# A seven-product MLP in fp32 on one core: the seventh product in split parts, a base block copied by GpSimd, the weights' sums held behind the tokens' square sums

## The chip, the cores and the metric

One core of a Trainium2 chip. The metric is device time in microseconds of one execution of the whole program (lower is better). Five engines run their own queues of instructions in order and wait for one another by semaphores: TensorE (PE), VectorE (DVE), ScalarE (ACT), GpSimd (POOL) and SyncE (SP), which here only issues transfers.

## The reference

A two-layer encoder trunk on 256 tokens of width 1024: layer 0 mixes tokens by neighbourhood and latent attention, layer 1 by dilated windows, and each is followed by an MLP with squared ReLU. All in float32.

```python
def sq_relu_mlp(xn, w1, w2):
    return jnp.square(jax.nn.relu(xn @ w1)) @ w2      # w1: 1024 x 4096, w2: 4096 x 1024

def reference(x, ...):
    for layer in range(2):
        xn = rms_norm(x, norm_mix[layer])
        x = x + (even_mixer if layer % 2 == 0 else odd_mixer)(xn, ...)
        x = x + sq_relu_mlp(rms_norm(x, norm_mlp[layer]), mlp_w1[layer], mlp_w2[layer])
    return rms_norm(x, norm_final)
```

## The kernel before

The tokens stay in SBUF, features on partitions (`x`, 8 blocks of 128 features by 256 tokens). The weights are streamed from HBM in chunks of up to 128 x 2048, in the order of one list (`specs`). The program has four phases in time: the even mixer, the first MLP, the odd mixer, the second MLP.

*Split products.* A float32 product is made of three passes in the format fp32r: each operand is split into a rounded part `hi` (a cast on ACT, L197) and the rest `lo` (a subtraction on DVE, L198), and `mm3` (L201 to L203) adds up hi x hi, hi x lo and lo x hi in PSUM. `split` does the one, `load_weight` and `split_piece` bring each chunk of weights: loads go up to four chunks ahead, splits up to two (`weight`). Three buffers hold split weights, four hold raw ones.

*The MLP* runs over 16 hidden chunks of 256. `up(j)` multiplies chunk j (48 matmuls of 128x256, weights stationary), then ReLU (L365) and square (L367). `down(j)` multiplies the hidden chunk by its second weights into eight PSUM banks of 128 tokens x 512 outputs. The order is up 0, 1, 2, down 0, up 3, down 1, and so on; a period is one up and one down. `beside` slips four transposes into some downs of the second MLP (L482).

*Seven products.* For the first 14 chunks the 2 x 2 x 2 block product (token halves x hidden halves x output halves) is done with seven products (`SEVEN`) instead of eight, after Strassen and Winograd. They need sums of hidden blocks (L373 to L375) and sums of blocks of weights. A weight chunk holds blocks 0, 1 and 2 as loaded; block 3 is the base of the sums:

- `sums` (two blocks): SP loads the base block into both (L139, 512 KB), then GpSimd issues a DMA that adds blocks 0 and 2 to them in memory (L140).
- `more_sums`: DVE adds block 0 to the second of the sums (L172, written over `raw`'s free fourth block) and block 1 to that (L173, the tile `every`).
- `split_sums` splits the two `sums` into `sumh` and `suml`, as one more step of `split_piece`.

Six products are three passes each. The seventh, Q4, is a single float32 matmul of `whole` (the unsplit square of one hidden block, L372) with the unsplit `every` (L389); the profile shows it as two matmuls. The last two chunks use plain products (`EIGHT`).

*The start of an MLP* is `hand_over`: for each quarter of the features, once its projection is done, DVE adds it to `x` (L300), ACT and DVE make `xh` and `xl` of the normed tokens (`prepare`, L237 and L238), and at the end `add_squares` forms the sums of squares of the tokens (L243 to L247). Their inverse root is applied after the down products, so TensorE can begin `up(0)` with the first quarters.

*Order.* Within these phases a scheduler sets each engine's order by the program's order, priorities and its own estimate of when inputs are ready; it can put an instruction ahead of earlier ones. `tc.high_priority` raises a block's instructions; `tc.issue_after(ins)` keeps a block's instructions on `ins`'s engine behind `ins`. On the engine itself the order is then fixed.

*Buffers that the change touches.* Tiles of tag `quarter` (four, shared with the mixers) hold the split hidden chunks `hh`; `hl` has three buffers of six blocks; `xt` (tokens first, 2 x 1024 columns) belongs to the last MLP.

Of the kernel before, what the change touches and what calls it, by code (L numbers as in the profile page):

```python
# [19 lines left out]
F32 = mybir.dt.float32  # L20
F32R = mybir.dt.float32r
AF = mybir.ActivationFunctionType
ALU = mybir.AluOpType
# [3 lines left out]
P = 128  # L27
D = 1024
KT = D // P
T = 256  # L30
NT = T // P
# [10 lines left out]
BLK = 512  # L42
# [7 lines left out]
def trunk(ctx, tc, a, out):  # L50
# [76 lines left out]
    plan_mlp(1)  # L127

    parts = {}
    state = {"loaded": 0, "split": (0, 0), "used": 0, "pool": None}  # L130

    def load_weight(pieces=1, before=lambda i: None):
        j = state["loaded"]
        src, n, _, seven = specs[j]
        if seven:

            blocks = src.rearrange("p (b n) -> p b n", n=BLK)
            sums = state["pool"].tile([P, 2, BLK], F32, tag="sum", name="sum", bufs=3)
            nc.sync.dma_start(sums, blocks[:, 3:4, :].broadcast_to([P, 2, BLK]))  # L139
            nc.gpsimd.dma_start(sums, blocks[:, 0:3:2, :], accum_op=ALU.add)  # L140
            n = 3 * BLK
        raw = wraw.tile([P, WCH], F32, tag="raw", name="raw")
# [11 lines left out]
    def split_piece(eng=None):  # L154
        j, i = state["split"]
        _, _, n, seven = specs[j]
        state["split"] = (j, i + 1) if i < n - (not seven) else (j + 1, 0)
        if i == 0:
            parts[j][1:3] = (wsp.tile([P, WCH], F32R, tag=v, name=v) for v in ("whi", "wlo"))
            if seven:  # L160
                more_sums(parts[j])
        if i == n:
            parts[j][1:3], (raw, hi, lo) = split_sums(parts[j])
            return split(hi, lo, raw)
        raw, hi, lo = (z[:, cut(j, i, n)] for z in parts[j][:3])
        return split(hi, lo, raw, eng)

    def more_sums(part):

        raw, sums = part[0].rearrange("p (b n) -> p b n", n=BLK), part[3]  # L170
        every = state["pool"].tile([P, BLK], F32, tag="every", name="every", bufs=2)
        nc.vector.tensor_tensor(raw[:, 3, :], sums[:, 1, :], raw[:, 0, :], op=ALU.add)  # L172
        nc.vector.tensor_tensor(every, raw[:, 3, :], raw[:, 1, :], op=ALU.add)  # L173
        part.append(every)

    def split_sums(part):
        _, hi, lo, sums, every = part
        more = [state["pool"].tile([P, 2, BLK], F32R, tag=v, name=v, bufs=2) for v in ("sumh", "suml")]
        blocks = lambda z, t: [z[:, b * BLK:(b + 1) * BLK] for b in range(4)] + [t[:, b, :] for b in range(2)]
        return [blocks(hi, more[0]) + [every], blocks(lo, more[1])], (sums, *more)  # L180

    def prefetch(loads, splits):
        while state["loaded"] < min(loads, len(specs)):
# [56 lines left out]
    def add_squares(b, s):  # L240

        q = scratch([2, T], "q") if b else two(s)
        nc.scalar.activation(q, x[:, 2 * b:2 * b + 2, :], AF.Square)  # L243
        if b:
            nc.vector.tensor_tensor(two(s), two(s), q, op=ALU.add)
        if b == 3:
            nc.vector.tensor_tensor(s[:, 0:T], s[:, 0:T], s[:, T:2 * T], op=ALU.add)  # L247

    def columns(s):

# [41 lines left out]
    def hand_over(accs, last, n):  # L292

        xT = half_tile(act, "xh", 2), half_tile(act, "xl", 2)
        s = sum_tile()
        for b in range(4):
            last[b]()
            v, acc = x[:, 2 * b:2 * b + 2, :], two(accs[b])
            with tc.high_priority(NORM_PRIO):
                nc.vector.tensor_tensor(v, acc, v, op=ALU.add)  # L300
                for f in zip(*(prepare(k, n, xT) for k in (2 * b, 2 * b + 1))):
                    done = [step() for step in f]

        with tc.issue_after(done[0]), tc.issue_after(done[1]):
            for b in range(4):
                add_squares(b, s)
        return xT, s

    def open_accs():
# [31 lines left out]

    SEVEN = (("P1", 5, 0), ("P2", 4, 1), ("Q3", 0, 2), ("Q6", 1, 3), ("Q5", 3, 4), ("Q7", 2, 5), ("Q4", None, 6))

    EIGHT = {"P2": ((1, 0), (0, 1)), "Q3": ((1, 3), (0, 2)), "C22": ((3, 3), (2, 2)), "Q4": ((3, 0), (2, 1))}

    def mlp(mp, xT, s, apart=(), beside=lambda j, p: None):

        hs = {}

        def up(j, pu):
            w = weight()

            ranges = [range(4), range(4, 6), range(6, 8)] if j == 0 else [range(8)]
            for ks in ranges:
# [6 lines left out]
            nc.scalar.activation(r, pu, AF.Relu)  # L365
            h = mp.tile([P, 8, P], F32, tag="h", name="h", bufs=1)
            nc.scalar.activation(h[:, 4:8, :].rearrange("p (t f) n -> p f t n", f=2), r.rearrange("p (f t n) -> p f t n", f=2, t=2), AF.Square)  # L367
            hh = act.tile([P, KT // 2, T], F32R, tag="quarter", name="hh", bufs=4).rearrange("p a (b n) -> p (a b) n", n=P)
            hl = mp.tile([P, 6, P], F32R, tag="hl", name="hl", bufs=3)
            if j < 14:  # L370
                whole = mp.tile([P, P], F32, tag="whole", name="whole", bufs=3)
                nc.scalar.activation(whole, r[:, P:2 * P], AF.Square)  # L372
                nc.vector.tensor_tensor(h[:, 2:4, :], h[:, 7:8, :].broadcast_to([P, 2, P]), h[:, 5:7, :], op=ALU.subtract)  # L373
                nc.vector.tensor_tensor(h[:, 1, :], h[:, 5, :], h[:, 3, :], op=ALU.subtract)
                nc.vector.tensor_tensor(h[:, 0, :], h[:, 4, :], h[:, 1, :], op=ALU.subtract)  # L375
                hs[j] = hh, hl, whole
                split(hh[:, 0:6, :], hl, h[:, 0:6, :])
            else:
                hs[j] = hh, hl
                split(hh[:, 0:4, :], hl[:, 0:4, :], h[:, 4:8, :])  # L380

        def down(j, m):
            wh, wl = weight()
            hh, hl, whole = hs[j]
            first = j == 0
            for n, i, b in SEVEN:
                end = j == 13 and (n not in EIGHT or n in apart)
                if n == "Q4":
                    nc.tensor.matmul(m[n], whole, wh[b], start=first, stop=end)  # L389
                else:  # L390
                    mm3(m[n], hh[:, i, :], hl[:, i, :], wh[b], wl[b], first, end)
                if n == "Q3":
                    beside(j, m["C22"])

        for j in range(3):
            up(j, bank("w"))
        inv = inverse_columns(s)
        m = {n: bank("w" if n in ("P1", "P2", "Q6", "C22") else "acc") for n in ("P1", "P2", "Q6", "C22", "Q7", "Q5", "Q3", "Q4")}
        for j in range(14):
            if j:  # L400
                up(j + 2, m["C22"])
# [68 lines left out]
    def finish(mp, xT, s):  # L470

        state["pool"] = mp
        HALF = [slice(0, 512), slice(512, D)]
        xt = mp.tile([P, NT, D], F32, name="xt")
        v = {(t, h): xt[:, t, HALF[h]] for t in range(NT) for h in range(2)}

        def tokens_first(j, pt):

            if j % 2 == 0 and 2 <= j < 10:
                t, h = divmod(j // 2 - 1, 2)  # L480
                for k in range(4):
                    nc.tensor.transpose(pt[:, k * P:(k + 1) * P], x[:, 4 * h + k, tok(t)], ident)  # L482
                nc.scalar.copy(v[t, h], pt)
# [650 lines left out]
```

## Time and profile before

| | |
|---|---|
| median of 3 runs | 754.21 us (753.8 to 755.93) |
| the profiled execution | 752.51 us, its span 750.7 us |
| granted TensorE clock, mean | 0.994 |
| DMA | 151.12 MB, mean 201 GB/s |
| first MLP | about 115 to 296 us of the span |
| second MLP | about 562 us to the end |

The profile is of one execution. Times in it are microseconds from the span's start. A group's row gives its line, engine and operation, output and inputs with their shapes, the count, then busy time, mean duration of one, and the engine's idle time just before with what ended it. Matmuls overlap, so their durations add up to more than the time they take; the distance between starts is what one costs. "PEld" is the load of a matmul's stationary operand, beside the matmuls. The chain is followed back from the last instruction, at each step to what released it.

### The profile page before, as it was taken

The page shows a single profiled execution, that of the slowest core. Times are in us where ns is not written, and L with a number is a line of the kernel's source. Part 1 is how long each engine was busy: PE and PEld are TensorE (multiplying, and loading weights), DVE is VectorE, ACT ScalarE, POOL GpSimd, SP SyncE. Part 2 cuts the span into 40 slices and gives each one's busy share as a digit, 9 for nine tenths or more (in the row PEclk, how much of TensorE's full clock was granted, in tenths as well). Part 3 has the DMA queues.
Part 4 walks back from the last instruction along what each step waited for, and adds up shares of the span by engine and source line. Part 5 has one row for each costly group of instructions (what it writes and reads, how often), then busy time and mean ns, then how long its engine had stood idle before and what let it go on. Part 6 is the DMA issues. An engine that isn't in the chain of part 4 may idle for free.

```text
span 750.7 us, 13847 instructions
## 1 busy us (share of the span) xinstructions
PE 734.1 (98%) x5414; PEld 677.3 (90%) x5414; DVE 583.5 (78%) x1062; ACT 542.8 (72%) x1027; POOL 38.9 (5%) x47
## 2 busy tenths in 40 slices
PE   9999998999999999999999999999997999999996
PEld 6988998988898888999999999999997988888885
DVE  6888858988788858877768777677766988778757
ACT  7778967757655666888988988889855757656752
POOL 0100001110111010000000000000010110010000
PEclk9999999999999999999999999999998999999999
DMA  8772348999999643633444444445668999999611
GB/s 314 277 265 107 113 140 213 302 282 268 272 274 280 191 146 146 237 144 131 180 173 141 165 145 155 155 141 169 224 209 185 264 271 266 263 273 261 195 60 56
DMA packets 37762, 151.12 MB, mean 201 GB/s; under 512 B 3776, under 2 KB 5312, under 8 KB 28608
## 3 DMA queue, kind: packets, MB, share of 16 engines
q1 hardware_dynamic: 29792, 135.28, 52.3%
q0 software_dynamic: 7616, 14.68, 11.5%
q8 instruction: 42, 0.69, 0.4%
q10 hardware_dynamic: 288, 0.28, 0.1%
q14 instruction: 24, 0.20, 0.1%
HBM read 149.18 MB, written 1.05 MB: 200 GB/s over the span
## 4 chain that ended last, share of the span: by engine, by line
PE 90%; DMA 4%; DVE 2%; ACT 2%; issue 1%; SPq 0%; POOL 0%; POOLq 0%; DVEq 0%
PE acc L201 15%; PE acc L202 15%; PE acc L203 15%; PE w L201 11%; PE w L202 11%; PE w L203 11%; DMA sum<-in_w 3%; PE acc L389 3%; PE w L210 1%; PE w L982 1%; PE w L964 1%; PE acc L997 1%; ACT whi L197 1%; PE w L798 1%; DVE wlo L198 1%
## 5 line engine op out<-in xcount | busy, mean ns | idle before, releaser
L198 DVE TENSOR_TENSOR wlo<-raw,whi 128x512 fp32r<-128x512 f32 (+3 forms) x360 | 297.3, 845 | 80.1 <-ACT whi L197 79.4
L197 ACT CAST whi<-raw 128x512 fp32r<-128x512 f32 (+3 forms) x360 | 253.4, 744 | 132.7 <-PE w L202 109.7
L201 PE MATMUL w<-xh,whi 128*128 128x256 f32 x528 | 160.3, 304 | 0.0
L202 PE MATMUL w<-xl,whi 128*128 128x256 f32 x528 | 150.3, 285 | 7.9 <-DVE xl L238 7.9
L203 PE MATMUL w<-xh,wlo 128*128 128x256 f32 x528 | 150.0, 284 | 0.0
L201 PE MATMUL acc<-xh,whi 128*128 128x256 f32 x432 | 125.2, 290 | 0.0
L202 PE MATMUL acc<-xl,whi 128*128 128x256 f32 x432 | 122.3, 283 | 0.0
L203 PE MATMUL acc<-xh,wlo 128*128 128x256 f32 x432 | 122.3, 283 | 0.0
L202 PEld LDWEIGHTS w<-xl,whi 128*128 128x128 f32 x528 | 102.0, 193 | 14.6 <-DVE xl L238 8.3
L201 PEld LDWEIGHTS w<-xh,whi 128*128 128x128 f32 x528 | 101.7, 193 | 6.3 <-issue 3.8
L203 PEld LDWEIGHTS w<-xh,wlo 128*128 128x128 f32 x528 | 102.0, 193 | 0.0
L201 PEld LDWEIGHTS acc<-xh,whi 128*128 128x128 f32 x432 | 82.6, 191 | 1.3 <-issue 0.3
L202 PEld LDWEIGHTS acc<-xl,whi 128*128 128x128 f32 x432 | 82.6, 191 | 0.0
L203 PEld LDWEIGHTS acc<-xh,wlo 128*128 128x128 f32 x432 | 82.6, 191 | 0.0
L140 POOL DMA_DIRECT2D sum<-in_w x28 | 30.7, 1095 | 531.5 <-PE acc L203 258.6
L201 PE MATMUL acc<-whi,xh 128*128 128x384 f32 (+2 forms) x160 | 55.5, 349 | 0.1
L202 PE MATMUL acc<-wlo,xh 128*128 128x384 f32 (+2 forms) x160 | 55.0, 344 | 0.4 <-DVE wlo L198 0.4
L203 PE MATMUL acc<-whi,xl 128*128 128x384 f32 (+2 forms) x160 | 54.7, 342 | 0.0
L201 PE MATMUL w<-whi,hh 128*128 128x512 f32 (+1 forms) x108 | 42.9, 398 | 0.0
L202 PE MATMUL w<-wlo,hh 128*128 128x512 f32 (+1 forms) x108 | 41.6, 385 | 0.0
L203 PE MATMUL w<-whi,hl 128*128 128x512 f32 (+1 forms) x108 | 41.3, 382 | 0.0
L931 DVE TENSOR_TENSOR r<-acc,cosT 128x512 f32<-128x512 f32 x24 | 16.6, 691 | 27.7 <-ACT sw L929 27.7
(225 smaller groups left out, 1422.8 us busy)
## 6 DMA issues: line engine op xcount, KB each, us to landing
raw<-in_w SPq DMA_DIRECT2D x36, 1024.0 KB, 6.2
raw<-in_w_oqk SPq DMA_DIRECT2D x24, 1024.0 KB, 4.9
raw<-in_w SPq DMA_DIRECT2D x28, 768.0 KB, 6.0
sum<-in_w SPq DMA_DIRECT2D x28, 512.0 KB, 7.9
sum<-in_w POOLq DMA_DIRECT2D x28, 512.0 KB, 9.3
raw<-in_w_ov SPq DMA_DIRECT2D x16, 768.0 KB, 4.3
raw<-in_w_oe SPq DMA_DIRECT2D x4, 1024.0 KB, 6.4
raw<-in_w_oo SPq DMA_DIRECT2D x4, 1024.0 KB, 4.8
```

The lines of the kernel that those rows point to most:

```text
L140: nc.gpsimd.dma_start(sums, blocks[:, 0:3:2, :], accum_op=ALU.add)
L197: a = nc.scalar.copy(hi, src).ins
L198: return a, (eng or nc.vector).tensor_tensor(lo, src, hi.bitcast(F32), op=ALU.subtract).ins
L201: nc.tensor.matmul(o, sh, mh, start=first, stop=False)
L202: nc.tensor.matmul(o, sh, ml, start=False, stop=False)
L203: nc.tensor.matmul(o, sl, mh, start=False, stop=last)
L210: nc.tensor.matmul(o[j], y[pb, 0, ts], z[pb, 1, :], start=n == 0, stop=n == 2)
L389: nc.tensor.matmul(m[n], whole, wh[b], start=first, stop=end)
L798: nc.tensor.transpose(pt[:, b * P:(b + 1) * P], pp[:, b // 2, (b % 2) * P:(b % 2 + 1) * P], ident)
L931: nc.vector.tensor_tensor(r1, pq.rearrange("p (f n) -> p f n", f=2), cosT.unsqueeze(1).broadcast_to([P, 2, T]), op=ALU.mult)
L964: nc.tensor.matmul(ss[i, j][rows, T:T + P], d["q12"][:, j, i * P + 64 * c:i * P + 64 * c + 64], d["k12"][:, j, 2 * i + c, :], start=True, ...
L982: nc.tensor.transpose(pt[:, b * P:(b + 1) * P], pp[:, b * P:(b + 1) * P], ident)
```

## The change

Four edits that go together:

1. `every` is split like the other sums (a third block of `sumh` and `suml`), hidden block 6 like the other hidden blocks (`hl` has seven blocks), and Q4 becomes three passes. The tile `whole` and its square on ACT go.
2. SP loads the base block into the first of the two `sums` alone (256 KB); GpSimd copies it into the second, then issues the accumulating DMA as before.
3. The two additions of `more_sums` are put behind the last addition of `add_squares` of the same MLP on DVE.
4. Buffers: one `every`; three `quarter` tiles taken once per MLP and used in turn; the fourth, in the last MLP, holds half of `xt`.

```diff
@@ load_weight
-            nc.sync.dma_start(sums, blocks[:, 3:4, :].broadcast_to([P, 2, BLK]))
+            nc.sync.dma_start(sums[:, 0, :], blocks[:, 3, :])
+            nc.gpsimd.tensor_copy(out=sums[:, 1, :], in_=sums[:, 0, :])
             nc.gpsimd.dma_start(sums, blocks[:, 0:3:2, :], accum_op=ALU.add)
@@ split_piece
             if seven:
-                more_sums(parts[j])
+
+                with tc.issue_after(state["parts_done"]):
+                    more_sums(parts[j])
         if i == n:
-            parts[j][1:3], (raw, hi, lo) = split_sums(parts[j])
-            return split(hi, lo, raw)
+            parts[j][1:3] = split_sums(parts[j])
+            return
@@ more_sums
-        every = state["pool"].tile([P, BLK], F32, tag="every", name="every", bufs=2)
+        every = state["pool"].tile([P, BLK], F32, tag="every", name="every", bufs=1)
@@ split_sums
-        more = [state["pool"].tile([P, 2, BLK], F32R, tag=v, name=v, bufs=2) for v in ("sumh", "suml")]
-        blocks = lambda z, t: [z[:, b * BLK:(b + 1) * BLK] for b in range(4)] + [t[:, b, :] for b in range(2)]
-        return [blocks(hi, more[0]) + [every], blocks(lo, more[1])], (sums, *more)
+        more = [state["pool"].tile([P, 3, BLK], F32R, tag=v, name=v, bufs=2) for v in ("sumh", "suml")]
+        split(*(t[:, 0:2, :] for t in more), sums)
+        split(*(t[:, 2, :] for t in more), every)
+        return [[z[:, b * BLK:(b + 1) * BLK] for b in range(4)] + [t[:, b, :] for b in range(3)] for z, t in zip((hi, lo), more)]
@@ add_squares
-            nc.vector.tensor_tensor(s[:, 0:T], s[:, 0:T], s[:, T:2 * T], op=ALU.add)
+            return nc.vector.tensor_tensor(s[:, 0:T], s[:, 0:T], s[:, T:2 * T], op=ALU.add).ins
@@ hand_over
-            for b in range(4):
-                add_squares(b, s)
+            state["parts_done"] = [add_squares(b, s) for b in range(4)][-1]
@@ mlp
-    SEVEN = (..., ("Q7", 2, 5), ("Q4", None, 6))
+    SEVEN = (..., ("Q7", 2, 5), ("Q4", 6, 6))
+        quarters = [act.tile([P, KT // 2, T], F32R, tag="quarter", name="hh", bufs=4) for _ in range(3)]
@@ up
-            hh = act.tile([P, KT // 2, T], F32R, tag="quarter", name="hh", bufs=4).rearrange("p a (b n) -> p (a b) n", n=P)
-            hl = mp.tile([P, 6, P], F32R, tag="hl", name="hl", bufs=3)
+            hh = quarters[j % 3].rearrange("p a (b n) -> p (a b) n", n=P)
+            hl = mp.tile([P, 7, P], F32R, tag="hl", name="hl", bufs=3)
             if j < 14:
-                whole = mp.tile([P, P], F32, tag="whole", name="whole", bufs=3)
-                nc.scalar.activation(whole, r[:, P:2 * P], AF.Square)
...
-                split(hh[:, 0:6, :], hl, h[:, 0:6, :])
+                split(hh[:, 0:7, :], hl, h[:, 0:7, :])
@@ down
-                if n == "Q4":
-                    nc.tensor.matmul(m[n], whole, wh[b], start=first, stop=end)
-                else:
-                    mm3(m[n], hh[:, i, :], hl[:, i, :], wh[b], wl[b], first, end)
+                mm3(m[n], hh[:, i, :], hl[:, i, :], wh[b], wl[b], first, end)
@@ finish, tokens_first
-        xt = mp.tile([P, NT, D], F32, name="xt")
+                    spare = act.tile([P, KT // 2, T], F32R, tag="quarter", name="xt0", bufs=4)
+                    xt.extend((spare.bitcast(F32).rearrange("p k n -> p (k n)"), mp.tile([P, D], F32, name="xt1")))
```

More of the change, by code (lines that the diff above doesn't have):

```diff
@@ L129, in trunk @@
     parts = {}
-    state = {"loaded": 0, "split": (0, 0), "used": 0, "pool": None}
+    state = {"loaded": 0, "split": (0, 0), "used": 0, "pool": None, "parts_done": None}
     def load_weight(pieces=1, before=lambda i: None):
@@ L336, in out_last @@
         return [lambda b=b: step(b) for b in range(4)]
-    SEVEN = (("P1", 5, 0), ("P2", 4, 1), ("Q3", 0, 2), ("Q6", 1, 3), ("Q5", 3, 4), ("Q7", 2, 5), ("Q4", None, 6))
+    SEVEN = (("P1", 5, 0), ("P2", 4, 1), ("Q3", 0, 2), ("Q6", 1, 3), ("Q5", 3, 4), ("Q7", 2, 5), ("Q4", 6, 6))
     EIGHT = {"P2": ((1, 0), (0, 1)), "Q3": ((1, 3), (0, 2)), "C22": ((3, 3), (2, 2)), "Q4": ((3, 0), (2, 1))}
@@ L367, in up @@
             nc.scalar.activation(h[:, 4:8, :].rearrange("p (t f) n -> p f t n", f=2), r.rearrange("p (f t n) -> p f t n", f=2, t=2), AF.Square)
-            hh = act.tile([P, KT // 2, T], F32R, tag="quarter", name="hh", bufs=4).rearrange("p a (b n) -> p (a b) n", n=P)
-            hl = mp.tile([P, 6, P], F32R, tag="hl", name="hl", bufs=3)
+            hh = quarters[j % 3].rearrange("p a (b n) -> p (a b) n", n=P)
+            hl = mp.tile([P, 7, P], F32R, tag="hl", name="hl", bufs=3)
+            hs[j] = hh, hl
             if j < 14:
-                whole = mp.tile([P, P], F32, tag="whole", name="whole", bufs=3)
-                nc.scalar.activation(whole, r[:, P:2 * P], AF.Square)
                 nc.vector.tensor_tensor(h[:, 2:4, :], h[:, 7:8, :].broadcast_to([P, 2, P]), h[:, 5:7, :], op=ALU.subtract)
@@ L375, in up @@
                 nc.vector.tensor_tensor(h[:, 0, :], h[:, 4, :], h[:, 1, :], op=ALU.subtract)
-                hs[j] = hh, hl, whole
-                split(hh[:, 0:6, :], hl, h[:, 0:6, :])
+                split(hh[:, 0:7, :], hl, h[:, 0:7, :])
             else:
-                hs[j] = hh, hl
                 split(hh[:, 0:4, :], hl[:, 0:4, :], h[:, 4:8, :])
@@ L383, in down @@
             wh, wl = weight()
-            hh, hl, whole = hs[j]
+            hh, hl = hs[j]
             first = j == 0
@@ L473, in finish @@
         HALF = [slice(0, 512), slice(512, D)]
-        xt = mp.tile([P, NT, D], F32, name="xt")
-        v = {(t, h): xt[:, t, HALF[h]] for t in range(NT) for h in range(2)}
+        xt = []
+        v = {}
         def tokens_first(j, pt):
@@ L480, in tokens_first @@
                 t, h = divmod(j // 2 - 1, 2)
+                if not xt:
+                    spare = act.tile([P, KT // 2, T], F32R, tag="quarter", name="xt0", bufs=4)
+                    xt.extend((spare.bitcast(F32).rearrange("p k n -> p (k n)"), mp.tile([P, D], F32, name="xt1")))
+                v[t, h] = xt[t][:, HALF[h]]
                 for k in range(4):
```

## The prediction

> **What bounds the kernel now.** I read the head of the page first (busy times and the chain that ended last), then the groups by shape, the order of TensorE's instructions in one period of the MLP, and the waits.
>
> ```profile
> PE 734.1 (98%) x5414; PEld 677.3 (90%) x5414; DVE 583.5 (78%) x1062; ACT 542.8 (72%) x1027; POOL 38.9 (5%) x47
> ...
> PE 90%; DMA 4%; DVE 2%; ACT 2%; issue 1%; SPq 0%; POOL 0%; POOLq 0%; DVEq 0%
> ```
>
> TensorE is busy 98% of the span and carries 90% of the chain. So an edit pays only if it shortens TensorE's own work, or closes one of the few gaps in it. The 4% of DMA on the chain are such gaps: the longest waits that concern them are
>
> ```profile
> DVE raw L172 <- DMA sum<-in_w: 8.4, 2, 5.3
> PE w L202 <- DVE xl L238: 7.9, 2, 5.1
> ...
> ACT sumh L197 <- DMA sum<-in_w: 6.2, 3, 3.4
> ```
>
> (total us, times, longest). TensorE waits 7.9 us in two places for `xl`, one at the start of each MLP; VectorE waits 8.4 us there for the sums of weights. In the other 26 downs VectorE does not wait for them at all, so in the running MLP the sums come early enough.
>
> **1. Q4 as three passes (TensorE).** Groups by shape, then one end of a down in order of time (start, duration), then the chain's pieces:
>
> ```profile
> L389 PE MATMUL acc<-every,whole 128*128 128x512 f32 x56 | 28.5, 591 | 0.0
> L201 PE MATMUL acc<-sumh,hh 128*128 128x512 f32 x56 | 21.8, 390 | 0.0
> ```
>
> ```profile
> 150.44 0.39 PE L201 MATMUL acc<-sumh,hh 128*128 128x512 f32 x1
> 150.67 0.39 PE L202 MATMUL acc<-suml,hh 128*128 128x512 f32 x1
> 150.90 0.39 PE L203 MATMUL acc<-sumh,hl 128*128 128x512 f32 x1
> 151.12 1.02 PE L389 MATMUL acc<-every,whole 128*128 128x512 f32 x2
> 151.58 0.69 PE L201 MATMUL w<-xh,whi 128*128 128x256 f32 x1
> 152.10 0.28 PE L202 MATMUL w<-xl,whi 128*128 128x256 f32 x1
> 152.22 0.28 PE L203 MATMUL w<-xh,wlo 128*128 128x256 f32 x1
> ```
>
> ```profile
> 140.57 0.86 PE acc L389 x2
> 151.28 0.86 PE acc L389 x2
> ```
>
> Matmuls overlap, so the price is the distance of starts, not the 390 or 591 ns of one. A three-pass product (Q7, the first three rows) takes 151.12 - 150.44 = 0.68 us. After Q4, the second matmul of the next up starts at 152.10, and these follow one another by 0.12, so the first belongs at 151.98: Q4 takes 151.98 - 151.12 = 0.86, as the chain says. The new Q4 has the shapes of Q7, hence 0.68. Gain 0.18 in a period that the chain puts at 151.28 - 140.57 = 10.71: it becomes 10.53. There are 28 downs; the last one's Q4 runs beside the tail, whose chain is already elsewhere:
>
> ```profile
> 728.97 0.59 ACT relu L365
> ```
>
> (the last Q4 comes at 732). 27 x 0.18 = **4.8 us**. Lower bound 0 (another engine becomes the period), upper 4.9.
>
> **2. What Q4's parts cost ACT and DVE.** Per down, a cast and a subtraction of 128x512 for `every`; the hidden blocks' split grows from 768 to 896 columns; ACT drops the square for `whole`.
>
> ```profile
> L198 DVE TENSOR_TENSOR wlo<-raw,whi 128x512 fp32r<-128x512 f32 x144 | 95.2, 684 | 17.2 <-ACT whi L197 17.0
> ...
> L198 DVE TENSOR_TENSOR hl<-h,hh 128x768 fp32r<-128x768 f32 x28 | 26.6, 950 | 0.0
> ```
>
> ```profile
> 172.71:183.42 10.71, 10.71 (x70) 9.51 (x69) 8.85 (x12) 6.78 (x10) 1.09 (x1) 1.00 0.98 286
> ```
>
> (a running period: length; busy PE, PEld, DVE, ACT, POOL; granted clock, DMA share, GB/s.) DVE adds 0.68 + 0.95 x 128/768 = 0.84: 9.7 of 10.53. ACT's share is bounded by DVE's prices for the same sizes, with nothing taken off for `whole`: 6.78 + 0.84 = 7.6. Both stay below TensorE, so this is hidden and I cost it at nothing; the cover is DVE's 0.8 us per period, and every 0.1 us above it would cost 28 x 0.1 = 2.8 us.
>
> **3. Base block once, copied by GpSimd.** SP moves 256 KB instead of 512 for each sum; GpSimd then copies 128x512 and only then issues the accumulating DMA. No row has this copy, so its bounds come from
>
> ```profile
> L874 POOL MEMSET k<- 128x1024 f32 x2 | 1.9, 951 | 38.1 <-DVE suml L198 22.4 <-DVE hl L198 15.8
> L745 POOL COPY ktok<-kpe 128x128 f32<-128x128 f32 x4 | 1.2, 293 | 39.5 <-DVE qk_l L198 30.8 <-PE acc L812 8.7
> ...
> L99 POOL MEMSET mean<- 128x128 f32 x1 | 0.2, 202 | 0.0
> ```
>
> ```profile
> sum<-in_w SPq DMA_DIRECT2D x28, 512.0 KB, 7.9
> sum<-in_w POOLq DMA_DIRECT2D x28, 512.0 KB, 9.3
> ```
>
> The memsets grow by (951-202)/896 = 0.84 ns a column, so a copy of 512 is about 293 + 384 x 0.84 = 0.61 us; four small copies would be 1.17. The load gains by its smaller half: between nothing and half of 7.9. So the sums land between 3.3 us earlier and 1.2 later; I take 0.3 later, nearer to the late end, since in program order the load stands behind 1 MB of raw weights on the same queue, whose bytes do not shrink. On POOL's queue only the sum's own accumulation and the next sums stand behind the copy. In the running MLP this is hidden (26 of 28 sums are not waited for). It matters at the two starts.
>
> **4. The sums held behind the square sums.** DVE (first two pairs), TensorE, then the chain, of the two starts:
>
> ```profile
> 119.99 0.69 DVE L172 TENSOR_TENSOR raw<-sum,raw 128x512 f32<-128x512 f32 x1 [3.15 <-DMA sum<-in_w]
> ...
> 121.74 1.66 DVE L238 SCALAR_TENSOR_TENSOR xl<-x,gains,xh 128x256 fp32r<-128x256 f32 x4
> ...
> 568.60 0.69 DVE L172 TENSOR_TENSOR raw<-sum,raw 128x512 f32<-128x512 f32 x1 [5.27 <-DMA sum<-in_w]
> ...
> 570.34 1.67 DVE L238 SCALAR_TENSOR_TENSOR xl<-x,gains,xh 128x256 fp32r<-128x256 f32 x4
> ```
>
> ```profile
> 122.27 0.39 PE L202 MATMUL w<-xl,whi 128*128 128x256 f32 x1 [2.78 <-DVE xl L238]
> ...
> 570.87 0.58 PE L202 MATMUL w<-xl,whi 128*128 128x256 f32 x1 [5.14 <-DVE xl L238]
> ...
> 574.88 0.33 PE L202 MATMUL w<-xl,whi 128*128 128x256 f32 x1
> ```
>
> ```profile
> 570.00:575.00 5.00, 4.13 (x19) 4.13 (x20) 5.00 (x10) 1.05 (x1) 0.00 (x0) 0.50 0.61 107
> ```
>
> L172, the first sum of weights, stands in VectorE's queue ahead of the last four `xl` and waits for its DMA; behind it `xl` waits, and TensorE with it. With L172 behind the last square sum, `xl` can run as soon as its `xh` is there, before TensorE asks for it. That frees 2.78 us at the first MLP and 5.14 at the second. The second gap also halves the granted clock: the 18 matmuls from 570.87 to 574.88 take 4.01 us instead of 18 x 0.12 = 2.16, another 1.85. Sum 9.8. The first gap costs no clock (its matmuls follow by 0.12 at once). The hold itself is an order within VectorE's queue; L172 and L173 then come behind the additions of the squares, by when their sum has landed. Behind them wait the subtractions of the sums' split and, over the freed buffers, SP's and GpSimd's next sums, none of which TensorE needs before the end of the first down.
>
> What is late next is ACT, where the cast of the second sum (not held) stands ahead of the first ReLU:
>
> ```profile
> 125.09 1.05 ACT L197 CAST sumh<-sum 128x1024 fp32r<-128x1024 f32 x1 [3.44 <-DMA sum<-in_w]
> 126.05 0.59 ACT L365 ACTIVATE relu<-w 128x512 f32<-128x512 f32 x1
> ...
> 132.49 0.95 DVE L198 TENSOR_TENSOR hl<-h,hh 128x768 fp32r<-128x768 f32 x1
> ```
>
> ```profile
> 136.34 0.34 PE w L201
> ...
> 586.81 0.34 PE w L201
> ```
>
> The first down needs that `hl`. Without the gap it begins at 136.34 - 2.78 = 133.6, and `hl` is done at 133.44 now, some 0.3 to 0.6 later with the copy: 0.2 to 0.5 us are given back. In the second MLP the down moves to 586.81 - 7.0 = 579.8; the cast there starts at 570.98, so ReLU could start at 572.0, with a sum 0.3 later at 572.3; `hl`, 7.4 us behind ReLU as in the first MLP, ends at 579.7, and 0 to 0.6 are given back. I take the upper ends, 1.1 for both, for the additional work on both engines.
>
> ```profile
> 570.98 1.05 ACT L197 CAST sumh<-sum 128x1024 fp32r<-128x1024 f32 x1 [1.28 <-DMA sum<-in_w]
> ```
>
> **5. Buffers.** One `every` instead of two is read by the split, not by TensorE, so it is free earlier. Three fixed quarters instead of four rotating: hidden chunk j+3 is written after down j by program order, as the three `hl` buffers demand already. Half of `xt` sits in the fourth quarter. Nothing for these; upwards bounded by one wait of a `hl` split, 0.95, per MLP.
>
> **Sum.** 4.8 + 2.8 + 5.1 + 1.85 - 1.1 = 13.5 us off the profiled execution's 752.51. That execution lies 1.7 below the median; the terms are differences, so they come off the median: 754.21 - 13.5 = **740.7 us**.
>
> **The rivals.**
> *The wait moves to ACT.* The casts of the sums are not held, and with the copy they may land later than I take. If the second sum comes 4 us later at both starts, ReLU, the first `hl` and the first down come about 3.5 us later each than forecast, and one of the two gaps halves the clock again (1.85): 740.7 + 2 x 3.5 + 1.85 = 749.6; half of it, 745. For it: ACT already waits 3.44 for that DMA. Against it: the load is half as large.
> *The hold only shifts the gap.* If the first down, not `xl`, sets the start, nothing of the 9.8 comes: 754.21 - 4.8 = 749.4. Against it: `hl` ended 2.9 us before the first down in the first MLP.
> *Slower: VectorE becomes the period.* GpSimd's copies and VectorE's subtractions may hold each other up, and VectorE's waits for ACT may not shrink. Its period is then 8.85 + 0.84 + 0.61 (a copy's length) + at most the idle 1.86 it has now = 12.2, 28 x 1.5 = 41 us more than now: 795 less the 8.7 of the starts, 786; with a fifth of that idle kept, 10.67 and about 744. It decides against the change from 10.71 + 8.7/28 = 11.02. Against it: without the idle, 10.3 is under 10.53.
> The Trainium skill, "SBUF — State Buffer", section "Who interferes with whom", speaks for this rival: a VectorE instruction with two SBUF inputs and a GpSimd instruction that reads SBUF cannot run at once, and the later one waits the whole of the other. No run here shows it (the four small copies lie beside instructions that read PSUM, or overlap by hardly anything).
> *No change* within 0.3% (2.3 us, about what a measurement of this kernel can tell): gains and losses of these rivals cancel.
>
> **Chances.** Forecast, 739 to 743.5: 0.63. ACT's wait: 0.16. Shifted gap: 0.07. VectorE's period at a small price, 743 to 751: 0.05. No change 0.03; slower 0.06, of which VectorE's period from 11.1 on is nearly all. Faster 0.91, same 0.03, slower 0.06. The range goes from all of the gain with nothing given back, 739.6 less a us of spread between runs, to the second rival's 749.4, less what is left out at both ends: 738.5 to 749.
>
> **What would show it.** Right: L389 has no matmul; Q4 is three passes of 0.23 and the period is 10.53; VectorE runs `xl` ahead of L172 at both starts; TensorE's wait for `xl` is gone and the granted clock stays 1.00; VectorE near 9.7 busy per period; GpSimd's copies near 0.6 us. Wrong: a gap in TensorE ahead of the first down that ACT's cast of a sum releases; a period above 10.53 with VectorE busy through it; copies of over 1.2 us, or VectorE's 128x512 above 684 ns in the MLPs.

## The result and the profile after

The changed kernel takes 737.97 us (median of 4 executions, 737.68 to 738.19) against 754.17 us of the kernel before on the same chip (4 executions, 753.8 to 755.93): 0.978 of the time, 95% interval 0.9763 to 0.9797. That is 16.2 us less by the medians. The prediction was 13.5 us less, 740.7, with a range from 738.5: right in direction and in what the gain comes from (Q4 and the hold), 2.7 us too little, and the time lies just below the range. The two profiled executions lie only 738.17 against 752.51, 14.3 us, apart. The difference between 16.2 and 14.3 turns out to be most of the error.

The head of the page after:

```profile
PE 727.2 (99%) x5442; PEld 680.7 (92%) x5442; DVE 610.5 (83%) x1090; ACT 558.9 (76%) x1027; POOL 79.9 (11%) x75
...
PE 92%; DVE 4%; ACT 1%; issue 1%; DMA 1%; POOL 0%; SPq 0%; POOLq 0%; DVEq 0%
```

The 4% of DMA on the chain have become 1%, and TensorE is now busy 99% of a shorter span. Its longest waits (engine, waiter and releaser: total us, times, longest) hold no `xl` any more:

```profile
PE acc L86 <- DVE warm L81: 1.2, 1, 1.2
PE acc L206 <- DVE wlo L202: 0.4, 2, 0.2
```

*Q4.* The same end of a down in order of time, the last seven-product rows before the next up:

```profile
148.19 0.39 PE L205 MATMUL acc<-sumh,hh 128*128 128x512 f32 x1
148.42 0.39 PE L206 MATMUL acc<-suml,hh 128*128 128x512 f32 x1
148.64 0.39 PE L207 MATMUL acc<-sumh,hl 128*128 128x512 f32 x1
148.87 0.28 PE L205 MATMUL w<-xh,whi 128*128 128x256 f32 x1
```

Q4 is three passes and takes 148.87 - 148.19 = 0.68 us. Its last row (L207, here at 148.64) stands at 159.18, 169.72 and 180.26 in the next downs: a period is 10.54 us.

*The hold.* VectorE's order at the two starts, then TensorE's first matmul that needs a late `xl`:

```profile
118.64 1.66 DVE L242 SCALAR_TENSOR_TENSOR xl<-x,gains,xh 128x256 fp32r<-128x256 f32 x4
...
124.49 0.42 DVE L251 TENSOR_TENSOR squares<-squares 128x256 f32<-128x256 f32 x1
124.82 0.69 DVE L175 TENSOR_TENSOR raw<-sum,raw 128x512 f32<-128x512 f32 x1
...
559.65 1.66 DVE L242 SCALAR_TENSOR_TENSOR xl<-x,gains,xh 128x256 fp32r<-128x256 f32 x4
...
565.84 0.68 DVE L175 TENSOR_TENSOR raw<-sum,raw 128x512 f32<-128x512 f32 x1
```

```profile
119.16 0.39 PE L206 MATMUL w<-xl,whi 128*128 128x256 f32 x1
```

The first sum of weights (L172 before, L175 now) stands behind the last square sum (L251), has no wait in brackets, and no longer holds `xl` up. The chain gives the time won at each station (the first downs, the end of the first MLP, the last ReLU):

```profile
133.58 0.34 PE w L205
279.36 0.50 PE w L432 x4
...
574.70 0.34 PE w L205
...
714.62 0.59 ACT relu L369
```

The first down begins 136.34 - 133.58 = 2.76 us earlier, close to the 2.78 of the first gap. At the end of the first MLP the chain before has 284.60, 5.24 later than the 279.36 here: the 2.76 and another 2.48, which is 14 times the 0.18 of Q4. The down in the second MLP begins 586.81 - 574.70 = 12.11 earlier, the last ReLU 728.97 - 714.62 = 14.35.

*VectorE and GpSimd.* One period and a stretch of ten of the running MLP (length; busy PE, PEld, DVE, ACT, POOL; granted clock, DMA share, GB/s), then two groups, the copy's among them, and the copy's durations (ns, shortest, median, longest):

```profile
175.53:186.06 10.53, 10.53 (x71) 9.69 (x71) 10.49 (x14) 7.42 (x9) 5.60 (x4) 1.00 0.86 223
145.00:250.00 105.00, 105.00 (x690) 96.66 (x689) 101.45 (x126) 74.20 (x92) 27.56 (x20) 1.00 0.91 258
```

```profile
L140 POOL COPY sum<-sum 128x512 f32<-128x512 f32 x28 | 41.4, 1494 | 468.3 <-DVE wlo L202 271.9 <-DMA sum<-in_w 142.6 <-ACT whi L201 21.8
L202 DVE TENSOR_TENSOR hl<-h,hh 128x896 fp32r<-128x896 f32 x28 | 32.5, 1160 | 0.0
```

```profile
L140 POOL COPY sum<-sum x28: 607/1183/4820, 108.8 to 676.9; 128x512 f32<-128x512 f32 x28
```

VectorE is busy 101.45 of 105, that is 10.17 of each period of 10.53, and not the 9.7 forecast. TensorE is still busy through all of it, so nothing is paid, but the cover has shrunk from 0.8 us to 0.36 in the mean, and to nothing in the single period shown.

### The profile page after: what moved, and what is told of

Read it like the earlier page. It is cut to its first block, busy times and chain, and to the rows that moved or that the text cites. A ratio compares the mean times of both kernels' runs of the same rounds, so it can differ in the third digit from the quotient of the medians.

```text
span 736.4 us, 14008 instructions
## 1 busy us (share of the span) xinstructions
PE 727.2 (99%) x5442; PEld 680.7 (92%) x5442; DVE 610.5 (83%) x1090; ACT 558.9 (76%) x1027; POOL 79.9 (11%) x75
## 4 chain that ended last, share of the span: by engine, by line
PE 92%; DVE 4%; ACT 1%; issue 1%; DMA 1%; POOL 0%; SPq 0%; POOLq 0%; DVEq 0%
PE acc L205 17%; PE acc L206 16%; PE acc L207 16%; PE w L205 11%; PE w L206 11%; PE w L207 11%; PE w L214 1%; PE w L985 1%; DVE wlo L202 1%; PE w L801 1%; PE w L967 1%; PE acc L1000 1%; PE w L815 1%; ACT whi L201 1%; DVE xl L242 1%
## 5 line engine op out<-in xcount | busy, mean ns | idle before, releaser
L207 PE MATMUL w<-xh,wlo 128*128 128x256 f32 x528 | 149.3, 283 | 0.0
L205 PE MATMUL w<-xh,whi 128*128 128x256 f32 x528 | 148.9, 283 | 0.0
L207 PE MATMUL acc<-xh,wlo 128*128 128x256 f32 x432 | 122.3, 283 | 0.0
L207 PEld LDWEIGHTS w<-xh,wlo 128*128 128x128 f32 x528 | 101.2, 192 | 0.0
L140 POOL COPY sum<-sum 128x512 f32<-128x512 f32 x28 | 41.4, 1494 | 468.3 <-DVE wlo L202 271.9
L207 PEld LDWEIGHTS acc<-xh,wlo 128*128 128x128 f32 x432 | 82.4, 191 | 0.0
L207 PE MATMUL acc<-whi,xl 128*128 128x384 f32 (+2 forms) x160 | 54.7, 342 | 0.0
L201 ACT CAST hh<-h 128x896 fp32r<-128x896 f32 (+1 forms) x32 | 28.9, 903 | 18.2 <-DVE h L378 17.2
L207 PE MATMUL w<-whi,hl 128*128 128x512 f32 (+1 forms) x108 | 41.2, 382 | 0.0
```

Source lines behind the costliest of these rows:

```text
L140: nc.gpsimd.tensor_copy(out=sums[:, 1, :], in_=sums[:, 0, :])
L201: a = nc.scalar.copy(hi, src).ins
L205: nc.tensor.matmul(o, sh, mh, start=first, stop=False)
L207: nc.tensor.matmul(o, sl, mh, start=False, stop=last)
```

## Experiments

The theories. CLOCK: a gap in TensorE's work can halve its clock or not, from execution to execution; the profiled execution of before is one in which the first gap did not, and the median is of executions in which it did. EARLY SUMS: with the copy the sums land earlier than taken, so nothing is given back at the starts. ORDER: nothing is given back because the order of the instructions changed, copy or no copy. BLOCKING: GpSimd's copy and VectorE's two-input instructions hold each other up, at a price that the starts show first. LONGER GAPS: in most executions the first gap is longer than in the trace. ELSEWHERE: what the medians gain beyond the traces comes from another part of the change. Against them stands the prediction's own sum.

**The kernel before again.** No edit.

> The kernel before, unchanged, to see the spread of its executions with the span and the granted clock of each. In its profiled execution (752.51 us, 1.7 under the median) the first gap cost no clock and the second 1.85 us. Theory CLOCK: whether a gap halves TensorE's clock, and for how long, differs from execution to execution; then the spans spread over some 752 to 756 us and the mean clock falls by about 0.0025 with each 1.85 us. Theory LONGER GAPS: outside the profiled execution the sums' transfers come later and the gaps are longer; the spans spread as much, the clock less than 0.001 beside the longer wait. Theory ELSEWHERE: the 1.9 us that the change gained beyond the trace (16.2 by medians, 14.3 between the two profiled executions) come from another part of the change; then the spread here is below 1 us around 754.

Measured: 754.02 us (752.66 to 755.57, 11 executions). With the other executions of before on this chip there are 34, which order themselves by the mean granted clock (the two middle rows overlap):

| mean clock | executions | us |
|---|---|---|
| 0.994 | 7 | 752.39 to 753.12 |
| 0.992 | 21 | 753.50 to 754.78 |
| 0.990 | 3 | 754.25 to 754.72 |
| 0.988 | 3 | 755.46 to 755.58 |

The execution on which the prediction rests (752.51 us, 0.994, from another session) would lie in the quickest fifth. The profiled one of this run is a typical one (0.992, 754.02 us). TensorE's timeline at the start of its first MLP, and the windows (this run, then the earlier trace):

```profile
122.58 0.58 PE L202 MATMUL w<-xl,whi 128*128 128x256 f32 x1 [2.84 <-DVE xl L238]
122.97 0.42 PE L203 MATMUL w<-xh,wlo 128*128 128x256 f32 x1
123.18 0.41 PE L201 MATMUL w<-xh,whi 128*128 128x256 f32 x1
...
125.53 0.33 PE L203 MATMUL w<-xh,wlo 128*128 128x256 f32 x1
125.70 0.28 PE L201 MATMUL w<-xh,whi 128*128 128x256 f32 x1
```

```profile
115.00:125.00 10.00, 7.16 (x51) 6.96 (x50) 6.80 (x13) 6.90 (x12) 1.09 (x1) 0.86 0.90 233
```

```profile
115.00:125.00 10.00, 7.22 (x60) 7.01 (x59) 6.85 (x12) 6.65 (x12) 1.17 (x2) 1.00 0.86 228
```

The gap is the same (2.84 and 2.78 us), but here the matmuls behind it follow by 0.21 instead of 0.12 for 3 us and the granted clock is 0.86 instead of 1.00. The first down begins at 137.94 instead of 136.34, 1.6 us later. LONGER GAPS falls by the equal gaps, ELSEWHERE by the spread of 3 us. So "the first gap costs no clock" is true of the execution forecast from and, by the mean clocks, false of most.

**Zeros in both gaps.** The kernel before, with matmuls of zeros added where TensorE waits for `xl`; they change no sum.

```diff
+        def zeros(pu, j, r):
+            for _ in range((20 if apart else 10) if j == 0 and r == 1 else 0):
+                nc.tensor.matmul(pu, warm[:, 0:P], warm, start=False, stop=False)
```

> The kernel before, with matmuls by a tile of zeros added onto the first up's bank just ahead of the matmuls that wait for xl: 10 in the first MLP (2.3 us at 0.23 each), 20 in the second (4.6 us). They keep TensorE busy in the gaps and make nothing else earlier. CLOCK: the halved clock after the gaps goes, about 1.85 us in the profiled execution and 3.7 in the median one: 750.5 us, all executions within 0.6 us, clock 0.997 or more. LONGER GAPS: only the 1.85 of the second gap comes: 752.3, spread as before. ELSEWHERE: 752.3 with a small spread. If the gap were set by TensorE itself the zeros would cost up to 6.9 us: 761.

Measured: 754.67 us (754.36 to 756.85, 12 executions), no gain, and not the 750.5 that CLOCK forecast. Eight of the executions have a clock of 0.998 or 0.999 and take 754.36 to 754.88; four have 0.996 and take 755.79 to 756.85. The profiled execution is one of the four: its second gap keeps the clock (1.00 from 560 to 580), but behind the first, of which 1.9 us stayed open, the matmuls follow by 0.21 from 123.9 to 127.1. And the added matmuls changed the scheduler's order on VectorE: TensorE then waited 1.8 us inside the second MLP's first down for `ms`, the instruction (L255) in which VectorE reads the tokens' sums of squares out of PSUM. So the total tells nothing of the price of the clock.

**The hold alone.** The kernel before, and of the change only edit 3.

```diff
             if seven:
-                more_sums(parts[j])
+                with tc.issue_after(state["parts_done"]): more_sums(parts[j])
...
+            state["parts_done"] = [add_squares(b, s) for b in range(4)][-1]
```

> The kernel before with the third edit alone: the two additions for the weights' sums held behind the tokens' square sums. The forecast's terms give 9.8 us less at most 1.1 given back: 744.4 to 745.5. CLOCK: the same gaps cost 1.9 more in the median execution, so 742.6, and all executions within 0.6 us. LONGER GAPS: 742.6 too. ELSEWHERE: 744.5. THE HOLD ONLY SHIFTS THE GAP (the forecast's rival): 754.

Measured: 743.72 us (743.44 to 743.87, 4 executions, clock 0.998 to 0.999) against 753.93: 10.2 us less. The executions now lie within 0.4 us, where those of before span 3.2. So the hold does more than shift the gap, which would have left 754. Not all is recovered: inside the first down of the second MLP, at its fourth product, TensorE waits again, for `ms` (by the program, that product and the sums of squares go into PSUM banks of one tag, `w`). CLOCK's 742.6 and this wait make 743.6.

```profile
579.81 0.49 PE L201 MATMUL w<-whi,hh 128*128 128x512 f32 x1 [0.99 <-DVE ms L255]
```

**Q4 alone.** The changed kernel without the hold and with the base block loaded twice by SP.

```diff
-                with tc.issue_after(state["parts_done"]):
-                    more_sums(parts[j])
+                more_sums(parts[j])
...
-            nc.sync.dma_start(sums[:, 0, :], blocks[:, 3, :])
-            nc.gpsimd.tensor_copy(out=sums[:, 1, :], in_=sums[:, 0, :])
+            nc.sync.dma_start(sums, blocks[:, 3:4, :].broadcast_to([P, 2, BLK]))
```

> Q4 in three passes with its splits and buffers alone; no hold, base block loaded twice as before. The forecast's term: 27 x 0.18 = 4.8, so 749.4 us; the profiled execution 747.7. CLOCK: the gaps and their spread of 2 to 3 us stay. ELSEWHERE, if the additional 1.9 us lie in the buffers or the order of the splits: 747.5.

Measured: 749.31 us (746.96 to 751.21, 6 executions), 4.6 less than 753.93. The term of 4.8 holds within the spread, which the two gaps, still there, keep wide.

**The change without the copy.** The hold and Q4; SP loads both base blocks (the second half of the diff above).

> The changed kernel with the base block loaded twice by SP, as before; no copy by GpSimd. The hold alone and Q4 alone add up to 10.2 + 4.6 = 14.8 us; the whole change gains 16.0. With the hold alone, TensorE still waits 0.99 us in the second MLP's first down (for ms); in the changed kernel it does not. Theory EARLY SUMS: the smaller load brings the first sums 0.5 us earlier and takes this wait away; without the copy it is back, 739.0 us. Theory ORDER: the wait is gone because Q4's parts put VectorE's queue in another order; 738.0. In both VectorE is less busy, 9.7 instead of 10.2 per period, which changes no time.

Measured: 738.49 us (738.10 to 738.79, 4 executions) against 754.55 in its own session: 0.978 of it, interval 0.9767 to 0.9793. That is 16.1 us against the 16.2 of the whole change, so the copy changes nothing in the total; the traces show a gain and, further below, a price of the same size. Here the wait inside the second MLP's first down is half of that with the hold alone, and VectorE has room again (the wait, `hl`'s group, the same stretch as above):

```profile
PE w L204 <- DVE ms L258: 0.5, 1, 0.5
```

```profile
L201 DVE TENSOR_TENSOR hl<-h,hh 128x896 fp32r<-128x896 f32 x28 | 30.5, 1090 | 0.0
```

```profile
145.00:250.00 105.00, 105.00 (x690) 96.63 (x690) 98.65 (x127) 74.10 (x92) 10.87 (x10) 1.00 0.96 285
```

EARLY SUMS and ORDER share it. This run and the changed kernel have the same order between `hl` and `ms` (2.72 and 2.73 us from the end of the one to the start of the other), but with the copy the cast of the second sum starts 10.35 us ahead of the down's first product (564.21, 574.56) instead of 8.48 (565.75, 574.23), and `hl` ends 1.58 us ahead of it instead of 0.13: that takes the last 0.5 away. With the hold alone L172 and L173 of the next chunk stand between `hl` and `ms` (3.00 us), and `hl` ends 0.12 after the first product has begun: 0.28 by the order and 0.25 by `hl` make the other half of the 0.99. VectorE's 98.65 of 105 is 9.89 a period: 0.2 more than forecast without the copy, and 0.28 on top with it.

**The change without the hold.** Q4 and the copy (the first half of the same diff).

> The changed kernel without the hold. The gaps come back, with the clock that they cost: 737.97 + 10.2 + 1.0 = 749.2 us, a little less (0.5 us for each gap) if the sums land earlier by the smaller load, so 748.2; spread over 2 us or more and clock 0.990 to 0.995 (theory CLOCK). If the copy itself, not the hold, had closed the gaps: 738 to 741.

Measured: 748.21 us (743.26 to 748.38, 6 executions): the hold is worth 748.21 - 737.97 = 10.2 in this kernel too (two chips). One kernel, 5 us between its executions: 743.26 has a clock of 0.998, the others 747.58 to 748.38 and 0.993 to 0.996. The 743.26 is the profiled one, and it has both gaps, 2.1 and 3.3 us, without a loss of clock. Its trace alone would have told that the hold is worth 5. How much of the 5 is clock and how much longer gaps in the others, no trace shows.

**Zeros in the first gap alone.** As above with 17 matmuls in the first gap and none in the second, to close it whole.

> The kernel before with 17 matmuls of zeros (3.9 us) in the first MLP's gap alone, enough to leave less than 0.5 us of it; the second gap stays as it is. CLOCK: no execution loses the clock in the first gap, so none lies in the groups of 0.988 to 0.992 by that gap: clock 0.994 in nearly all, and the time that of the fastest group before, 752.7, plus up to 1 us if the zeros overrun the gap or the queues come in another order. If the executions differ for another reason, the groups 0.994 to 0.988 and the spread of 3 us stay.

Measured: 756.97 us (755.49 to 758.15, 10 executions), and not the 752.7 forecast. The first gap is closed and keeps its clock, but again VectorE's order changed: L172 of the next chunk waits 1.47 us for its `raw` and `ms` stands behind it. So inside the first down there is a new gap, which in this execution halves the clock itself:

```profile
141.60 0.50 PE L201 MATMUL w<-whi,hh 128*128 128x512 f32 x1 [2.17 <-DVE ms L255]
...
143.10 0.63 PE L203 MATMUL acc<-sumh,hl 128*128 128x512 f32 x1
143.53 0.63 PE L201 MATMUL acc<-sumh,hh 128*128 128x512 f32 x1
143.96 0.63 PE L202 MATMUL acc<-suml,hh 128*128 128x512 f32 x1
```

Rows that follow by 0.23 elsewhere follow by 0.43. The total is inconclusive; a gap of 2.2 us was enough here.

**The copy twice.** The changed kernel, each base block copied two times by GpSimd.

```diff
-            nc.gpsimd.tensor_copy(out=sums[:, 1, :], in_=sums[:, 0, :])
+            [nc.gpsimd.tensor_copy(out=sums[:, 1, :], in_=sums[:, 0, :]) for _ in range(2)]
```

> The changed kernel with GpSimd's copy made twice for each sum (the same bytes again). In the changed kernel a copy takes 0.61 us alone and 1.49 in the mean, and VectorE is busy 10.17 of each 10.5 us. Theory BLOCKING: a copy and VectorE's two-input instructions hold each other up, each copy costs VectorE up to 0.45 us; with two it needs 10.4 to 10.7, at the edge of the period: 738 to 742 us, copies over 1.5 us in the mean, VectorE's sums of hidden blocks longer than before. Theory NO BLOCKING: the copies only take GpSimd's time and memory's; VectorE's durations stay, 738.0.

Measured: 742.2 us (741.63 to 743.25, 5 executions): 4.2 us for 28 more copies (two sessions), just above what BLOCKING expected at most. VectorE needs 10.40 us a period (103.75 in the same stretch of 105), as expected, but TensorE stays busy through it: the price is paid mostly at the starts. The first MLP begins its first down 1.74 us later (135.18 against 133.44) and ends as much later (281.10 - 279.36); the second begins its own 3.40 later (577.96 against 574.56), and the last ReLU comes 718.68 - 714.62 = 4.06 later. The rows: TensorE's wait, then VectorE and GpSimd at the first start.

```profile
PE w L206 <- DVE xl L242: 1.8, 5, 0.5
```

```profile
114.47 3.65 DVE L242 SCALAR_TENSOR_TENSOR xl<-x,gains,xh 128x256 fp32r<-128x256 f32 x3
```

```profile
114.43 1.56 POOL L140 COPY sum<-sum 128x512 f32<-128x512 f32 x2
115.75 1.30 POOL L141 DMA_DIRECT2D sum<-in_w  x1
116.49 1.34 POOL L140 COPY sum<-sum 128x512 f32<-128x512 f32 x1
```

Three `xl` of some 0.4 us each take 3.65 us while GpSimd copies. ACT had all their `xh` ready at 114.95, so they did not wait for inputs. In the changed kernel the first four `xl` take 2.46 us (from 113.93) beside single copies, against 1.69 in the kernel before. No wait for `xl` is listed, but it is not free: from the start of these `xl` to the first product of the first down (its first `hh` row, 133.44) it takes 19.51 us, against 19.17 with the hold alone and in the change without the copy. At the second start it is 19.39 against 19.23 in both. So BLOCKING stands: in the periods the changed kernel has cover for it, at the starts it pays 0.34 + 0.16 = 0.5 us, as much as the earlier sums win.

**The hold at one start.** The kernel before with edit 3 in the first MLP alone, then in the second alone, on one chip: the direct test of term 4, gap by gap.

```diff
+                with tc.issue_after(state["parts_done"]) if j < len(specs) // 2 else nullcontext(): more_sums(parts[j])
```

> The kernel before with the hold in the first MLP alone, so that only the first gap (2.78 us for xl) closes. By the prediction's term (the first gap costs its length and no clock): 754.2 - 2.8 = 751.4. CLOCK (the first gap also halves the clock in most executions, worth another 1.5): 749.9, and the executions lie within about 1 us of each other, since what varied is gone; mean clock 0.994 in nearly all.

> The kernel before with the hold in the second MLP alone, so that the second gap closes and the first stays. By the prediction's terms: 754.2 - 5.14 - 1.85 = 747.2, plus about 0.9 that the run with both holds still waited there, 748.1, and all executions alike, since the gap that halved the clock is gone. CLOCK: the same median, but the executions still fall into groups some 1.5 us apart (about 746.5, 748, 749.5) that go with mean clocks from 0.998 down to 0.994. The gains of this run and of the one with the first hold should add up to the 10.2 of both holds.

Measured: with the first alone 749.60 us (749.20 to 750.16, 6 executions), with the second alone 748.26 (746.81 to 748.37, 6), before 754.14 (11). The first gap is worth 754.14 - 749.60 = 4.5 us in the median and not 2.8. The 95% interval is wide, 2.7 to 6.0, because before spreads over 5 us here; but none of the six reaches the 751.4 that the prediction's term gives, and they lie within 1 us, as CLOCK expects. The second is worth 5.9 (4.4 to 7.4); together 10.4, against 10.2 with both holds. TensorE's waits and the first start of the run with the second hold:

```profile
PE w L202 <- DVE xl L238: 2.8, 1, 2.8
...
PE w L201 <- DVE ms L255: 1.1, 1, 1.1
```

```profile
115.00:125.00 10.00, 7.21 (x52) 7.01 (x51) 6.84 (x13) 6.55 (x12) 1.23 (x2) 0.89 0.85 224
```

Here too the first gap of 2.8 us lowers the clock (0.89). By the same measure as above (first four `xl` to the first product of the first down) the start takes 19.17 us with the first hold, 22.23 in the trace that was forecast from, where the gap cost no clock, and 23.75 here and 23.59 in the run of the kernel before, where it did. So the gap is worth 3.06 without the clock and 4.4 to 4.6 with it, which is the 4.5 of the medians. Five of the six executions with the second hold take 747.90 to 748.37 at 0.996; the one at 0.998 takes 746.81. The third group that CLOCK expected, 749.5, did not appear. So the first gap's clock is worth about 1.5 us and is lost in most executions.

## Why the prediction was right and wrong

*Term 1, Q4: right.* 0.68 us per product, periods of 10.54, 4.6 measured against 4.8.

*Term 2, "hidden": right, but for too small a number.* VectorE needs 10.17 us a period and not 9.7. A part (0.2) comes without the copy; half of that because the stretch of ten periods took 8.94 a period before (87.67 of 105), where the forecast went by the 8.85 of one. The rest (0.28) comes from the copy.

*Term 3, the copy: mis-sized, without a net price.* Alone it takes 0.61 us, as worked out from the memsets and the small copies; over all 28 its mean is 1.49 and its longest 4.82. Both signs that the prediction names for this (copies of over 1.2 us, VectorE's 128x512 above 684 ns) are there. The longest in its place, GpSimd and then VectorE:

```profile
172.62 4.78 POOL L140 COPY sum<-sum 128x512 f32<-128x512 f32 x1 [8.02 <-DMA sum<-in_w]
```

```profile
172.91 0.68 DVE L176 TENSOR_TENSOR every<-raw 128x512 f32<-128x512 f32 x1
173.51 1.08 DVE L202 TENSOR_TENSOR hl<-h,hh 128x896 fp32r<-128x896 f32 x1
174.51 1.22 DVE L202 TENSOR_TENSOR suml<-sum,sumh 128x1024 fp32r<-128x1024 f32 x1
175.65 0.68 DVE L202 TENSOR_TENSOR suml<-every,sumh 128x512 fp32r<-128x512 f32 x1
176.25 0.68 DVE L175 TENSOR_TENSOR raw<-sum,raw 128x512 f32<-128x512 f32 x1
176.97 0.98 DVE L176 TENSOR_TENSOR every<-raw 128x512 f32<-128x512 f32 x1
```

The copy lasts through five two-input instructions of VectorE that follow one another at once, and ends in the sixth (172.62 + 4.78 = 177.40), whose 0.98 instead of 0.68 shows the delay on the other side. By the Trainium skill, "SBUF — State Buffer", section "Who interferes with whom", the two cannot run at once and the later one waits for the whole of the other. The trace agrees: the copy began while a `wlo` of VectorE ran (171.78, 1.22 us long). It adds that a chain of VectorE instructions keeps the copy out for longer than one of them. So the mechanism of the slower rival is there in every period; it did not decide because the period had 0.8 us of room and needed 0.5 of it. At the starts, where there is no room, the copy costs 0.5 us and its earlier sums win 0.5.

*Term 4, the hold: the two steps that failed.* The mechanism of the hold and both lengths were right: the start gains are 2.76 and, in the second MLP, 12.11 - 2.76 - 14 x 0.18 (the Q4 of the first MLP) = 6.83 of the 6.99 forecast. Wrong was

1. "The first gap costs no clock", and with it "they come off the median". The terms are differences of one execution, and in that execution the first gap had cost less than in most. The hold at the first start alone is worth 4.5 us in the median, 1.7 more than the term of 2.78: 0.3 because the gap costs a little more than its listed length (3.06), and some 1.4 for the clock. The 1.7 by which the profiled execution lay below the median was mostly this clock, not an offset common to both kernels; afterwards it is gone.
2. "I take the upper ends, 1.1 for both". ACT was to give this back: with the cast of the second sum ahead of the first ReLU, and the sum 0.3 us later, `hl` would be late for the first down. Neither holds in the changed kernel (ACT and VectorE, first MLP, then second):

```profile
123.08 0.59 ACT L369 ACTIVATE relu<-w 128x512 f32<-128x512 f32 x1
123.56 1.04 ACT L201 CAST sumh<-sum 128x1024 fp32r<-128x1024 f32 x1
...
129.64 1.09 DVE L202 TENSOR_TENSOR hl<-h,hh 128x896 fp32r<-128x896 f32 x1
...
564.21 1.05 ACT L201 CAST sumh<-sum 128x1024 fp32r<-128x1024 f32 x1 [1.35 <-DMA sum<-in_w]
...
571.90 1.08 DVE L202 TENSOR_TENSOR hl<-h,hh 128x896 fp32r<-128x896 f32 x1
```

At the first start ReLU now stands ahead of the cast (with the hold alone too: 122.61 and 124.91). At the second it stands behind, but the sum comes earlier, not later: 570.98 less the 5.24 won by then is 565.74, and the cast starts at 564.21. So `hl` ends 2.7 and 1.6 us before the first product of the down (133.44 and 574.56). Of 9.77 forecast ahead of the 1.1, 2.76 + 6.83 = 9.59 came: 0.2 less, where 1.1 was taken. What was given back went to the copy, which holds up `xl` on VectorE (0.34 and 0.16), and not to ACT. The wait that the hold alone leaves (0.99) has another cause too, `ms` on VectorE; one half of it is gone by the copy's earlier sums, the other by VectorE's order and an earlier `hl`.

By the traces the gain is 14.3 and not 13.5, 0.8 more; the profiled execution of before lay 1.7 below its median, and that of the changed kernel lies 0.2 above its own: 2.7 us. The lower end of the range, 738.5, allowed for nothing given back and one us of spread, and had no room for the 1.7. By parts: 4.6 (Q4 alone) + 4.5 (first hold) + 5.9 (second hold), as medians, + 1.1 (the wait for `ms` in the trace with the second hold, which the changed kernel does not have) - 0.5 (the copy at the starts) = 15.6, against 16.2 measured. These medians have intervals of 2.5 to 3.3 us, so the 0.6 is not resolved.

*Term 5, buffers: right.* No wait for them shows.

*The rivals.* The wait did not move to ACT: no idle time of TensorE stands ahead of the first downs or in them. The hold did not only shift the gap, and the period is not VectorE's.

## What to carry to other kernels

A trace is one execution: before a gap is costed from it, see where its own time and mean clock lie among the other executions, and whether a gap of this length has cost clock elsewhere; in these runs a gap of some 2 to 3 us was worth its length and often another 1.5 us, and closing it narrowed the spread as well. An instruction that waits for a DMA is to stand behind those in the same queue that TensorE needs. A copy given to GpSimd is free only while VectorE has slack for it: cost it at what it takes beside VectorE's two-input work, and keep it away from the start of a stage.

## What the runs showed of the hardware

*The clock.* Gaps of 2.78 and 2.84 us at the same place left the granted clock at 1.00 in one execution and took it to 0.86 in another; one of 2.17 us and one of 1.9 us (the runs with zeros) halved the rate behind them; gaps of 2.1 and 3.3 us in one execution cost none. The time at the halved rate is about 3 us at the first start: 122.58 to 125.53 in one run, right behind the gap, and 123.9 to 127.1 in another, where the gap had ended at 122.51. The Trainium skill, "TensorE: Matmul & The Clock Gate", section "What's actually happening", has a window of about 3.4 us that runs freely and after which an idle array is throttled, so that the point of change depends on where in the window the work falls. That the outcome varies from execution to execution and the start of the slow stretch from run to run fits it; that a gap of 1.9 us can suffice does not fit a whole idle window, and here the measurement decides. What fixes the outcome in one execution was not found.

*The shared access of VectorE and GpSimd.* A 128x512 copy on GpSimd took 0.61 us alone, 1.49 in the mean and 4.82 at most beside VectorE's two-input instructions; these went from 0.68 to as much as 1.10 (L176), and three `xl` beside three copies took 3.65 us.
